# TensorE's instructions in phase 1 of a gated-DeltaNet layer: the scheduler's order against the order of emission

## The chip, the cores and the metric

One core of one Trainium2 chip runs the whole layer as one program. The metric is the device time of one execution in microseconds; for a profiled execution the profile also gives a span, from the first instruction of the core to the last.

## The reference, cut to what matters

One decoder layer, batch 1, 256 tokens, width 2048, everything in float32. The first half is the gated DeltaNet:

```python
mod = cond @ mod_w + mod_b                      # six vectors of 2048: sh1, sc1, ga1, sh2, sc2, ga2
h = x * (1 + sc1) + sh1
proj = h @ w_in                                 # 256 x 2048 by 2048 x 12352: q, k, v, z, beta, a
qkv = silu(causal_depthwise_conv(qkv, conv_w))  # 4 taps
q, k = l2norm(q) * 128 ** -0.5, l2norm(k)       # 16 heads of 128; v, z have 32 heads
# per value head, chunks of 64 in the reference (the kernel takes 128):
L = strict_lower((k * beta) @ k.T * decay)
u, w = solve(L + I, [v * beta, k * beta * exp(gc)])
# state recurrence over the chunks gives o
o = o * rsqrt(mean(o * o)) * norm_w * silu(z)
y = o @ w_out                                   # 4096 -> 2048
x = layer_norm(alpha * x + (1 + ga1) * y)
y = (silu(h2 @ w_gate) * (h2 @ w_up)) @ w_down  # SwiGLU, 5632 wide
out = layer_norm(alpha * x + (1 + ga2) * y)
```

## The kernel before, in words

**Products.** Every big matrix product is done in "groups" of 512 output columns (class `Group`, L194). A group walks over the 16 k-tiles of 128 in chunks of four. Each f32 weight tile is split into a rounded high part and a rest: ScalarE writes `wh` (L190), VectorE writes `wl` (L191), each 128 x 1024, for two k-tiles at once. One k-tile for one half `t` of the tokens is three matmuls of 512 columns (L223 to L225), here called three products. So a group is 96 products and one pair `wh`, `wl` serves 12 of them. There are four buffers each of `raw`, `wh` and `wl`, which is 48 products of lead. The variable `pos` counts chunks: one unit of it is 24 products. All times given to tasks are in this unit.

**Phases.** First come the modulation vectors and six groups that are interleaved with them (`first`), whose accumulators have the name `gd`. Phase 1 is the rest of the projection `w_in`: the loop over q = 1 to 3 (q, k and two v groups each) and the z groups, accumulators `pj`. Then the output projection (`oTa` and so on), the SwiGLU and the second norm follow. The change is in phase 1.

**Tasks.** Beside the products of phase 1 the kernel does the convolution and the DeltaNet for four batches q = 0 to 3 of eight value heads each. These are Python generators that `spawn` puts in a heap with a time in `pos`. `advance(t)`, called ahead of every three products, emits those steps that are due; `yield d` puts the rest of a task off by d. A task's step emits instructions on TensorE, VectorE, ScalarE and others at once. The steps that the prediction speaks of:

- `conv_silu`: four transposes into `tp` (L462), on VectorE six shifted multiply-adds `cy` (L470), Silu; later `qk_pair` transposes back (L494), `v_pair` (L529).
- `gates`: emitted once, ahead of phase 1. Transposes (L415), some twenty small VectorE and ScalarE operations ending in `q` (L443), then two matmuls (L445, L446).
- `la_task`: four per batch. ScalarE writes `dg` (L543), TensorE transposes it (L547), ScalarE takes the exponent `dm` (L551), TensorE multiplies k by k and q (L556), VectorE scales into `LA` (L561).
- `solve_task`: one per batch. ScalarE copies the diagonal blocks (L570), VectorE transposes them to `LD` (L573), then inverts 32 x 32 triangles in 31 dependent pairs of small operations (`tmp` L584, `X` L586) and transposes back to `XD` (L588). After a `yield` of SOLVE = 5.4 the small matmuls L600, L601 on `XD` follow, then further products (L608 to L627) with `yield HOP` between them.
- `state_task`: two per batch, matmuls L640 to L685, a `yield HOP` between most steps.
- `mods_late`: streams 96 tiles `mraw` of 128 x 1024 and adds each to `macc` on VectorE (L272, the first of 32 by L271), one per 0.95 `pos`; its sums go through L351 and L280.

**What sets the order.** Each engine runs its instructions in the order of its program, and waits at an instruction until what it needs is there. That order is made when the kernel is built. `at(p)` gives what is emitted inside it the priority p: lower first. A list scheduler goes through modelled time and gives each engine, whenever it is free, the ready instruction of lowest priority number. So an instruction of a task whose operand is late in the model lets products pass, and it comes on the engine when its operand is there in the model. The weight splits have a priority ten `pos` ahead (`SPLIT`) and so go before everything else as soon as a buffer is free.

Of the kernel before, what the change touches and what calls it, by code (L numbers as in the profile page):

```python
# [18 lines left out]
KT = D // 128  # L19
FF = 5632  # L20
FT = FF // 128
NQ = 4
# [7 lines left out]
def gdn_layer_kernel(ctx: ExitStack, tc: tile.TileContext, x, c, mod_w, mod_b, ln_g, ln_b,  # L30
# [3 lines left out]

    SPLIT, MOD0, MODEVERY = 10, 30.0, 0.95
    MGAP, CGAP0, CGAP, CSTEP = 1.5, 1.0, 2.0, 2.3
    CONV, PAIR, SILU = 0.2, 0.4, 2.4
    GDN, LAGAP, LA1, LA2, LA3, SOLVE, HOP = 3.0, 0.5, 0.3, 0.6, 1.5, 5.4, 0.6
    ALONE, MACW, ZW, OW = 1.5, 1.0, 0.1, 0.3


# [26 lines left out]
    def spawn(t, gen):  # L68
        heappush(tasks, (t, len(seq), gen))
        seq.append(gen)  # L70
# [3 lines left out]
    def drain(but=None):  # L74
        while any(x_[2] is not but for x_ in tasks):
            advance(now[0] + 0.1)

    def advance(t):
        now[0] = t
        while tasks and tasks[0][0] <= t:  # L80
            t0, i, gen = heappop(tasks)
            with at(t0):
                d = next(gen, None)
            if d is not None:
                heappush(tasks, (t0 + d, i, gen))
# [16 lines left out]
    w_in2 = w_in.rearrange("l k n -> (l k) n")  # L102
# [74 lines left out]
    pos = [0]  # L177
# [299 lines left out]
    def evac(t, ps):  # L477
        n = gp.tile([128, 512], F32, name="nat", tag="nat", bufs=4)
        act(n, ps, AF.Copy)
        return n  # L480

    def qk_pair(q, which, nat, h, ss, both):
        ct0 = (16 if which == 0 else 0) + q * 4
        while q > 1 and q - 2 not in state_ends:
            yield 0.2
        if q not in kq:
            kq[q] = gp.tile([128, 4, 2, 256], F32, name="kq", tag="kq", bufs=2)
        if which == 0 and q not in knat:
            knat[q] = gp.tile([128, 4, 128], F32, name="knat", tag="knat", bufs=2)
        yield from conv_silu(nat, h, ct0 + h, kq[q][:, h:h + 2, which, :])  # L490
        p = tp()
        for c in range(2):
            for i in range(2):
                tr(p[:, c * 256 + i * 128:c * 256 + (i + 1) * 128],  # L494
                   kq[q][:, h + i, which, c * 128:(c + 1) * 128], ident)
        if which == 0:
            act(knat[q][:, h:h + 2, :], p[:, 0:256].rearrange("p (a b) -> p a b", a=2), AF.Copy)
        for c in range(2):
            for i in range(2):
                src = p[:, c * 256 + i * 128:c * 256 + (i + 1) * 128]  # L500
                act(src, src, AF.Square, accum_out=ss[:, c, h + i:h + i + 1])
        both.append(h)

    def qk_norm(q, which, ss, both):
        while len(both) < 2:
            yield 0.2
        ts(ss, ss, NORM_EPS, None, op0=OP.add)
        r = work.tile([128, 2, 4], F32, name="rn", tag=f"rn{which}", bufs=2)
        nc.gpsimd.tensor_tensor(r.rearrange("p a b -> p (a b)"), ss.rearrange("p a b -> p (a b)"),
                                mhalf[:, 0:8], op=OP.pow)  # L510
        r2 = work.tile([128, 2, 4, 2], F32, name="rr", tag=f"rr{which}", bufs=2)
        ts(r2, r[:, :, :, None].to_broadcast([128, 2, 4, 2]), 1.0 if which == 0 else QSCALE, None, op0=OP.mult)
        (rk2 if which == 0 else rq2)[q] = r2.rearrange("p a b c -> p a (b c)")
        if which == 0:
            i2 = work.tile([128, 2, 4, 2], F32, name="ik", tag="ik", bufs=2)
            tt(i2, r2, ss[:, :, :, None].to_broadcast([128, 2, 4, 2]), op=OP.mult)
            ik2[q] = i2.rearrange("p a b c -> p a (b c)")
        return
        yield

    def v_pair(q, half, nat, h):
        ct0 = 32 + q * 8 + half * 4
        vT = yield from conv_silu(nat, h, ct0 + h, None)
        while q not in ik2:
            yield 0.2
        p = tp()
        for c in range(2):
            for i in range(2):
                tr(p[:, c * 256 + i * 128:c * 256 + (i + 1) * 128], vT[:, i, c * 128:(c + 1) * 128], ident)  # L529
        hq = half * 4 + h  # L530
        for c in range(2):
            for i in range(2):
                act(oq[q][:, c, hq + i, :], p[:, c * 256 + i * 128:c * 256 + (i + 1) * 128], AF.Copy,
                    scale=ik2[q][:, c, hq + i:hq + i + 1])
# [156 lines left out]
    def gdn(q):  # L691


        while q not in rq2 or q and q - 1 not in state_ends:
            yield 0.2
        hv, rk, rq = q * 8, rk2[q], rq2[q]
        LA[q] = gp.tile([128, 16, 2, 128], F32, name="LA", tag="LA", bufs=1)
        sc = work.tile([128, 2, 2, 8], F32, name="gsc", tag="gsc", bufs=2)
        tt(sc[:, 0], rk, rk, op=OP.mult)
        tt(sc[:, 0], sc[:, 0], beta[:, :, hv:hv + 8], op=OP.mult)  # L700
        tt(sc[:, 1, 0], sc[:, 0, 0], kse[:, hv:hv + 8], op=OP.mult)
        for c in range(2):
            for g in range(2):
                spawn(now[0] + LAGAP * (2 * c + g), la_task(q, c, g, sc))
        yield 3 * LAGAP + LA3
        yield from solve_task(q)
        omq[q] = work.tile([128, 2, 8], F32, name="om", tag="om", bufs=2)
        spawn(now[0] + 0.3, state_task(q, 1, sc))
        yield from state_task(q, 0, sc)
        while state_done.get(q) != 2:  # L710
            yield 0.1
        state_ends.add(q)
        f = work.tile([128, 2, 8], F32, name=f"fo{q}", tag=f"fo{q}", bufs=1)
        t = work.tile([128, 2, 8], F32, name="ft", tag="ft", bufs=1)
        tt(t, rq, rq, op=OP.mult)
        tt(t, t, omq[q], op=OP.mult)
        ts(t, t, 1.0 / 128.0, NORM_EPS, op0=OP.mult, op1=OP.add)
        nc.gpsimd.tensor_tensor(f.rearrange("p a b -> p (a b)"), t.rearrange("p a b -> p (a b)"), mhalf, op=OP.pow)
        tt(f, f, rq, op=OP.mult)
        fo[q] = f  # L720
# [3 lines left out]
    def conv_start():  # L724
        t = max(now[0] + CONV, conv_free[0])
        conv_free[0] = t + CSTEP
        return t

    def qk_done(q, which):
        nat = []  # L730

        def done(t, ps, n=None):
            nat.append(evac(t, ps) if n is None else n)
            if t == 0:
                return
            both = []
            ss = work.tile([128, 2, 4], F32, name="ss", tag="ss", bufs=2)
            t1 = conv_start()
            for h in (0, 2):
                spawn(t1 + PAIR / 2 * h, qk_pair(q, which, nat, h, ss, both))  # L740
            spawn(t1 + PAIR + SILU + 0.6, qk_norm(q, which, ss, both))
        return done

    def v_done(q, half):
        nat = []

        def done(t, ps, n=None):
            nat.append(evac(t, ps) if n is None else n)
            if t == 0:
                return  # L750
            if q not in oq:
                oq[q] = held.tile([128, 2, 8, 128], F32, name=f"oq{q}", tag=f"o{q}")
            t1 = conv_start()
            for h in (0, 2):
                spawn(t1 + PAIR / 2 * h, v_pair(q, half, nat, h))
            if half == 1:
                spawn(t1 - CONV + GDN, gdn(q))
        return done
# [149 lines left out]
    def late_mods():  # L908
        yield from mods_late(ga1, 32, 1.0, MODEVERY)
        yield from mods_late(sc2, 64, 1.0, MODEVERY)  # L910
        yield from mods_late(sh2, 48, 0.0, MODEVERY)
        tt(A2, lng[:, 0:KT], sc2, op=OP.mult)
        tt(B2, lnb[:, 0:KT], sc2, op=OP.mult)
        tt(B2, B2, sh2, op=OP.add)
# [3 lines left out]
    mods_gen = late_mods()  # L918
    spawn(MOD0, mods_gen)

    def z_group(q, half):
        Group(w_in2, 8192 + q * 1024 + half * 512, h_hi, h_lo, KT, z_done(q, half)).run()

    for q in range(1, NQ):
        if q > 1:
            Group(w_in2, 2048 + q * 512, h_hi, h_lo, KT, qk_done(q, 0)).run()
            Group(w_in2, q * 512, h_hi, h_lo, KT, qk_done(q, 1)).run()
        for half in range(2):
            Group(w_in2, 4096 + q * 1024 + half * 512, h_hi, h_lo, KT, v_done(q, half)).run()
        if q == 1:  # L930
            z_group(0, 0)
    for z in range(1, 2 * NQ):
        z_group(z // 2, z % 2)
    z1 = pos[0]
    drain(mods_gen)

    with at(z1 - 2):
        r = [held.tile([128, D], F32, name=f"r{t}", tag=f"h{t}") for t in range(2)]
# [194 lines left out]
```

## Time and profile before

| | us |
|---|---|
| median of 3 runs | 1722.5 (1720.7 to 1725.71) |
| the profiled execution | 1725.16 |
| its span | 1723.4 |
| TensorE busy | 1668.0 (97% of the span) |
| VectorE busy | 1139.7 (66%) |
| ScalarE busy | 882.0 (51%) |
| DMA, mean | 227 GB/s |

Matmuls overlap in the pipeline (a product is listed with some 390 to 400 ns and the next starts after 228 ns), so TensorE's busy share says that it seldom waits, not that it is at its peak. Phase 1 lies between about 218 and 780 us.

### The profile page before, as it was taken

Reading aid. Unit: us, or ns where it says so; the run is one execution under the profiler, and the core shown is the slowest. Engines: PE = TensorE matmul, PEld = TensorE weight load, DVE = VectorE, ACT = ScalarE, POOL = GpSimd, SP = SyncE. Lnnn points to the kernel's source line nnn. Section 1 sums busy time; section 2 is a strip of 40 time slices with the busy share of each in tenths; the row PEclk is TensorE's granted clock in tenths of the full one; section 3 lists DMA queues with packets and bytes.
Section 4 is the critical chain, followed back from the end, with each engine's and each line's share of the span. In section 5 each row is a group of like instructions: output and inputs, shape, how many; then the busy total and the mean of one; then the engine's idle time right before and its main releaser. Section 6 shows DMA issues by size and latency. Waiting matters only on the chain.

```text
span 1723.4 us, 23269 instructions
## 1 busy us (share of the span) xinstructions
PE 1668.0 (97%) x8685; PEld 1325.3 (77%) x8685; DVE 1139.7 (66%) x1635; ACT 882.0 (51%) x1430; POOL 61.2 (4%) x66
## 2 busy tenths in 40 slices
PE   5999999999999999999999999999999999999996
PEld 2666778787887878788787788888878887888885
DVE  2466988958966988847776865865467544455455
ACT  2433669769568667564333744444444443433332
POOL 0000000001001000000000000000000000000003
PEclk8999999999999999999999999999999999999998
DMA  9998786535864777747888586886678666756662
GB/s 347 364 338 286 223 283 191 170 112 159 255 204 117 241 251 241 245 147 238 302 278 282 158 270 185 304 268 189 189 246 284 191 185 207 249 192 192 196 193 101
DMA packets 184082, 390.82 MB, mean 227 GB/s; under 512 B 12112, under 2 KB 14592, under 8 KB 182944
## 3 DMA queue, kind: packets, MB, share of 16 engines
q1 hardware_dynamic: 181952, 378.64, 67.7%
q0 software_dynamic: 2016, 10.68, 1.8%
q8 instruction: 68, 1.11, 0.3%
q14 instruction: 46, 0.38, 0.1%
HBM read 385.08 MB, written 4.19 MB: 226 GB/s over the span
## 4 chain that ended last, share of the span: by engine, by line
PE 70%; DVE 12%; DMA 7%; ACT 5%; issue 4%; POOL 1%; SPq 1%; POOLq 0%; DVEq 0%; ACTq 0%
PE pj L223 19%; PE pj L225 19%; PE pj L224 19%; DMA mraw<-in_mod_w_dram 6%; DVE wl L191 5%; ACT wh L190 2%; PE gd L225 1%; PE gd L224 1%; DVE macc L272 1%; DVE cy L470 1%; PE gd L223 1%; DVE X L586 1%; DVE tmp L584 1%; PE tp L311 1%; PE tp L1039 1%
## 5 line engine op out<-in xcount | busy, mean ns | idle before, releaser
L191 DVE TENSOR_TENSOR wl<-raw,wh 128x1024 fp32r<-128x1024 f32 x522 | 635.1, 1222 | 376.7 <-ACT wh L190 374.1
L190 ACT ACTIVATE wh<-raw 128x1024 fp32r<-128x1024 f32 x522 | 552.3, 1061 | 602.4 <-PE pj L225 481.1
L223 PE MATMUL pj<-wh,h2T 128*128 128x512 f32 x704 | 278.2, 395 | 0.0
L225 PE MATMUL pj<-wh,h2T 128*128 128x512 f32 x704 | 276.7, 393 | 0.0
L224 PE MATMUL pj<-wl,h2T 128*128 128x512 f32 x704 | 276.5, 393 | 0.0
L223 PE MATMUL pj<-wh,hT 128*128 128x512 f32 x640 | 256.8, 403 | 0.0
L224 PE MATMUL pj<-wl,hT 128*128 128x512 f32 x640 | 256.5, 401 | 0.1
L225 PE MATMUL pj<-wh,hT 128*128 128x512 f32 x640 | 256.2, 401 | 0.0
L272 DVE SCALAR_TENSOR_TENSOR macc<-mraw,cond,macc 128x1024 f32<-128x1024 f32 x120 | 153.6, 1280 | 54.6 <-DMA mraw<-in_mod_w_dram 53.9
L223 PEld LDWEIGHTS pj<-wh,h2T 128*128 128x128 f32 x704 | 132.8, 189 | 30.5 <-issue 1.6
L225 PEld LDWEIGHTS pj<-wh,h2T 128*128 128x128 f32 x704 | 132.7, 189 | 28.7 <-issue 0.8
L224 PEld LDWEIGHTS pj<-wl,h2T 128*128 128x128 f32 x704 | 132.7, 188 | 27.8 <-issue 0.8
L223 PEld LDWEIGHTS pj<-wh,hT 128*128 128x128 f32 x640 | 120.8, 189 | 26.7 <-issue 3.3
L224 PEld LDWEIGHTS pj<-wl,hT 128*128 128x128 f32 x640 | 120.8, 189 | 24.5 <-DVE wl L191 0.9
L225 PEld LDWEIGHTS pj<-wh,hT 128*128 128x128 f32 x640 | 120.9, 189 | 24.4 <-issue 1.2
L470 DVE SCALAR_TENSOR_TENSOR cy<-tp,cw,cy 128x255 f32<-128x255 f32 (+2 forms) x192 | 86.2, 476 | 1.3 <-ACT cy L466 1.2
L224 PE MATMUL gd<-wl,hT 128*128 128x512 f32 x128 | 51.5, 404 | 1.4 <-DVE wl L191 1.4
L223 PE MATMUL gd<-wh,hT 128*128 128x512 f32 x128 | 49.9, 398 | 2.0 <-DVE part L256 1.1
L225 PE MATMUL gd<-wh,hT 128*128 128x512 f32 x128 | 51.8, 408 | 0.0
L311 PE MATMUL tp<-mraw,cond 128*32 128x256 f32 x368 | 34.9, 464 | 11.4 <-DMA mraw<-in_mod_w_dram 11.4
L223 PE MATMUL pj<-wh,oTc 128*128 128x512 f32 x112 | 43.9, 392 | 0.0
L225 PE MATMUL pj<-wh,oTc 128*128 128x512 f32 x112 | 43.8, 391 | 0.0
(388 smaller groups left out, 2266.3 us busy)
## 6 DMA issues: line engine op xcount, KB each, us to landing
raw<-in_gdn_w_in_dram SPq DMA_DIRECT2D x194, 512.0 KB, 4.6
mraw<-in_mod_w_dram SPq DMA_DIRECT2D x192, 512.0 KB, 5.4
raw<-in_ffn_w_gu_dram SPq DMA_DIRECT2D x176, 512.0 KB, 4.3
raw<-in_ffn_w_down_dram SPq DMA_DIRECT2D x88, 512.0 KB, 4.6
raw<-in_gdn_w_out_dram SPq DMA_DIRECT2D x64, 512.0 KB, 5.1
x<-in_x_dram SPq DMA_DIRECT2D x8, 256.0 KB, 5.9
r<-in_x_dram POOLq DMA_DIRECT2D x2, 1024.0 KB, 5.0
x1s<-r POOLq DMA_DIRECT2D x2, 1024.0 KB, 6.8
```

The costliest lines, as they stand in the source:

```text
L190: act(hi, raw, AF.Copy)
L191: tt(lo, raw, f32(hi), op=OP.subtract)
L223: mm(ps, sh, wh, start=start, stop=False)
L224: mm(ps, sh, wl, start=False, stop=False)
L225: mm(ps, sl, wh, start=False, stop=stop)
L272: return stt(acc, w, cond[:, k:k + 1], acc, op0=OP.mult, op1=OP.add)
L311: mm(p[32 * j:32 * j + 32, 0:hw], cond[:, k:k + 1].to_broadcast([128, 32]), raw[:, kl, j * hw:(j + 1) * hw], start=(k == 0), stop=(k == KT ...
L470: stt(y[:, o + s:o + 256], p[:, o:o + 256 - s], tap(3 - s, ct + i), y[:, o + s:o + 256], op0=OP.mult, op1=OP.add)
L584: tt(tv, LD[:, j + 1:32, j:j + 1].to_broadcast([128, n, m]), X[:, j, None, 0:m].to_broadcast([128, n, m]), op=OP.mult)
L586: tt(X[:, j + 1:32, 0:m], X[:, j + 1:32, 0:m], tv, op=OP.subtract)
L1039: tr(p[:, i * 256 + t * 128:i * 256 + (t + 1) * 128], nats[j, t][:, (2 * i2 + i) * 128:(2 * i2 + i + 1) * 128], ident)
```

## The change

The region `manual_schedule` for TensorE is put around the loops of phase 1. Inside it TensorE's instructions keep the order in which they are emitted: all of a step's TensorE instructions stand in one place, at the `pos` at which the task was due, and the products behind them stay behind them. The other engines are ordered by the scheduler as before. Four constants of the task times are changed too: the convolution starts 0.45 instead of 0.2 `pos` after its group, LA1 goes from 0.3 to 0.5, HOP from 0.6 to 0.7. SOLVE stays at 5.4.

```diff
-    CONV, PAIR, SILU = 0.2, 0.4, 2.4
-    GDN, LAGAP, LA1, LA2, LA3, SOLVE, HOP = 3.0, 0.5, 0.3, 0.6, 1.5, 5.4, 0.6
+    CONV, PAIR, SILU = 0.45, 0.4, 2.4
+    GDN, LAGAP, LA1, LA2, LA3, SOLVE, HOP = 3.0, 0.5, 0.5, 0.6, 1.5, 5.4, 0.7
...
-    for q in range(1, NQ):
...
-    z1 = pos[0]
-    drain(mods_gen)
+
+    with tc.manual_schedule(engines={mybir.EngineType.PE}):
+        for q in range(1, NQ):
+            if q > 1:
+                Group(w_in2, 2048 + q * 512, h_hi, h_lo, KT, qk_done(q, 0)).run()
+                Group(w_in2, q * 512, h_hi, h_lo, KT, qk_done(q, 1)).run()
+            for half in range(2):
+                Group(w_in2, 4096 + q * 1024 + half * 512, h_hi, h_lo, KT, v_done(q, half)).run()
+            if q == 1:
+                z_group(0, 0)
+        for z in range(1, 2 * NQ):
+            z_group(z // 2, z % 2)
+        z1 = pos[0]
+        drain(mods_gen)
```

What this moves is seen in the order of the built programs. The first place is TensorE at the start of phase 1, where the gates are computed; L415 writes the transposes that the chain of small operations starts from, L445 takes that chain's result `q`. Before, around L415 and then around L445, with 83 products between the two:

```order
L223 MATMUL pj<-wh,hT_116 128x512
L415 MATMUL tp<-ident,bT 128x64 x2
L224 MATMUL pj<-wl,hT_116 128x512
L225 MATMUL pj<-wh,hT_118 128x512
```

```order
L224 MATMUL pj<-wl,hT_117 128x512
L225 MATMUL pj<-wh,hT_119 128x512
L445 MATMUL tp<-q,upper 128x64
L446 MATMUL tp<-q,upper 128x32
L462 MATMUL tp<-ident,part 128x128 x4
L223 MATMUL pj<-wh,hT_117 128x512
```

The same place in the change, where the last row ahead of L415 is the last product of the six first groups:

```order
L223 MATMUL gd<-wh,hT_117 128x512
L224 MATMUL gd<-wl,hT_117 128x512
L225 MATMUL gd<-wh,hT_119 128x512
L415 MATMUL tp<-ident,bT 128x64 x2
L445 MATMUL tp<-q,upper 128x64
L446 MATMUL tp<-q,upper 128x32
L462 MATMUL tp<-ident,part 128x128 x4
L223 MATMUL pj<-wh,hT_116 128x512
L224 MATMUL pj<-wl,hT_116 128x512
```

No product stands between L415 and L445 any more: the first convolution of the region (L462) comes behind L446 as it did before, and the products of the region come behind that convolution.

The second place is VectorE ahead of the second `XD` (batch q = 1). Before, the end of that inversion with the weight splits and convolutions between its pairs:

```order
L272 SCALAR_TENSOR_TENSOR macc<-mraw,cond,macc 128x1024
L586 TENSOR_TENSOR X<-X,tmp 128x6x13
L470 SCALAR_TENSOR_TENSOR cy<-tp,cw_102,cy 128x255
L584 TENSOR_TENSOR tmp<-LD,X 128x70
L470 SCALAR_TENSOR_TENSOR cy<-tp,cw_102,cy 128x255
L586 TENSOR_TENSOR X<-X,tmp 128x5x14
L191 TENSOR_TENSOR wl<-raw,wh 128x1024
L584 TENSOR_TENSOR tmp<-LD,X 128x56
L191 TENSOR_TENSOR wl<-raw,wh 128x1024
L586 TENSOR_TENSOR X<-X,tmp 128x4x14
```

And in the change, the end of the same inversion:

```order
L584 TENSOR_TENSOR tmp<-LD,X 128x56
L272 SCALAR_TENSOR_TENSOR macc<-mraw,cond,macc 128x1024
L586 TENSOR_TENSOR X<-X,tmp 128x4x14
L584 TENSOR_TENSOR tmp<-LD,X 128x45
L272 SCALAR_TENSOR_TENSOR macc<-mraw,cond,macc 128x1024
L586 TENSOR_TENSOR X<-X,tmp 128x3x15
L584 TENSOR_TENSOR tmp<-LD,X 128x30
L586 TENSOR_TENSOR X<-X,tmp 128x2x15
L584 TENSOR_TENSOR tmp<-LD,X 128x16
L586 TENSOR_TENSOR X<-X,tmp 128x16
L588 STREAM_TRANSPOSE XD<-X 128x32x16
```

The last weight split of this stretch now stands some 36 rows ahead of `XD`, and `macc` stands where splits and convolutions stood.

The third place is TensorE at the same solve, between the last L556 of the batch's four la tasks and the first L600. Before, 283 products stand between the two, and the L600s may cut a group of three:

```order
L224 MATMUL pj<-wl,hT_116 128x512
L225 MATMUL pj<-wh,hT_118 128x512
L223 MATMUL pj<-wh,hT_116 128x512
L224 MATMUL pj<-wl,hT_116 128x512
L225 MATMUL pj<-wh,hT_118 128x512
L223 MATMUL pj<-wh,hT_116 128x512
L600 MATMUL gd<-XD,LA 32x32
L601 MATMUL gd<-XD,LA 32x32
```

In the change 141 products stand between the two, in whole threes, with six steps of four transposes (the last an L529) and one pair of L351 and L280:

```order
L529 MATMUL tp<-ident,cy 128x128 x4
L223 MATMUL pj<-wh,hT_117 128x512
L224 MATMUL pj<-wl,hT_117 128x512
L225 MATMUL pj<-wh,hT_119 128x512
L223 MATMUL pj<-wh,hT_117 128x512
L224 MATMUL pj<-wl,hT_117 128x512
L225 MATMUL pj<-wh,hT_119 128x512
L223 MATMUL pj<-wh,hT_117 128x512
L224 MATMUL pj<-wl,hT_117 128x512
L225 MATMUL pj<-wh,hT_119 128x512
L600 MATMUL gd<-XD,LA 32x32
L601 MATMUL gd<-XD,LA 32x32
```

The solve moved ahead by 142 products relative to its la tasks. For the four batches the number of products between the last L556 and the first L600 goes from 228, 283, 255 and 230 to 138, 141, 138 and 174. Between the same marks VectorE's program (from the first of the last four L561 to L588) holds, before: 18, 23, 21, 19 splits `wl`; 42, 36, 36, 0 multiply-adds `cy`; 0, 11, 7, 8 `macc` of L272. In the change: 11, 12, 13, 15 splits; 24, 12, 24, 0 `cy`; 0, 13, 11, 5 `macc`. Over the whole program the places at which TensorE goes from a product to something else go from 308 to 286.

## Rows read from the trace of the kernel before

**Rows 1.** The page's part 1, TensorE: busy us (share of the span), instructions.

```profile
PE 1668.0 (97%) x8685; PEld 1325.3 (77%) x8685; DVE 1139.7 (66%) x1635; ACT 882.0 (51%) x1430; POOL 61.2 (4%) x66
```

**Rows 2.** TensorE's waits at 212 to 790 us: total us, times, longest us.

```profile
PE tp L445 <- DVE q L443: 2.5, 1, 2.5
...
PE gd L600 <- DVE XD L588: 2.1, 3, 1.7
```

**Rows 3.** TensorE's timeline in phase 1: start us, us, what, count.

```profile
422.20 0.40 PE L223 MATMUL pj<-wh,hT 128*128 128x512 f32 x1
...
422.58 0.66 PE L462 MATMUL tp<-ident,nat 128*128 128x128 f32 x4
...
422.99 0.48 PE L224 MATMUL pj<-wl,hT 128*128 128x512 f32 x1
...
424.61 0.39 PE L225 MATMUL pj<-wh,hT 128*128 128x512 f32 x1
...
431.89 0.39 PE L224 MATMUL pj<-wl,hT 128*128 128x512 f32 x1
```

**Rows 4.** Stretches from last L556 step to first L600, one per batch.

```profile
core 0: us, PE busy (x) PEld busy (x) DVE busy (x) ACT busy (x) POOL busy (x), PEclk, DMA share, GB/s
290.67:351.93 61.26, 60.34 (x287) 48.06 (x286) 54.99 (x137) 46.51 (x105) 3.27 (x2) 1.00 0.54 156
411.20:485.30 74.10, 73.24 (x349) 58.50 (x348) 71.13 (x151) 47.97 (x92) 4.24 (x2) 1.00 0.77 243
541.18:609.59 68.41, 66.77 (x321) 53.16 (x319) 65.03 (x143) 46.43 (x97) 3.27 (x2) 1.00 0.71 221
668.20:725.03 56.83, 55.11 (x251) 45.31 (x249) 55.38 (x118) 29.42 (x33) 0.00 (x0) 1.00 0.80 255
```

**Rows 5.** VectorE's groups, first of these stretches: busy us, mean ns | idle.

```profile
L191 DVE TENSOR_TENSOR wl<-raw,wh 128x1024 fp32r<-128x1024 f32 x19 | 23.2, 1224 | 4.5 <-ACT wh L190 4.4
...
L470 DVE SCALAR_TENSOR_TENSOR cy<-tp,cw,cy 128x255 f32<-128x255 f32 (+2 forms) x42 | 19.8, 481 | 0.0
```

**Rows 6.** The same in the second stretch.

```profile
L191 DVE TENSOR_TENSOR wl<-raw,wh 128x1024 fp32r<-128x1024 f32 x23 | 27.9, 1218 | 0.4 <-ACT wh L190 0.3
...
L470 DVE SCALAR_TENSOR_TENSOR cy<-tp,cw,cy 128x255 f32<-128x255 f32 (+2 forms) x36 | 17.1, 475 | 0.0
...
L272 DVE SCALAR_TENSOR_TENSOR macc<-mraw,cond,macc 128x1024 f32<-128x1024 f32 x12 | 15.3, 1274 | 0.4 <-DMA mraw<-in_mod_w_dram 0.4
```

**Rows 7.** TensorE's timeline around the gates.

```profile
219.49 0.33 PE L415 MATMUL tp<-ident,bT 64*128 64x64 f32 x2
...
241.31 0.41 PE L445 MATMUL tp<-q,upper 128*128 128x64 f32 x2 [2.45 <-DVE q L443]
```

**Rows 8.** VectorE's timeline of the gates: first and last of 29 rows.

```profile
220.58 0.28 DVE L417 COPY ba<-tp 128x128 f32<-128x128 f32 x1
...
240.95 0.22 DVE L443 SCALAR_TENSOR_TENSOR q<-q,nA 128x64 f32<-128x64 f32 x1
```

**Rows 9.** A stretch with la tasks; columns as in rows 4.

```profile
245.00:300.00 55.00, 54.95 (x274) 44.28 (x273) 47.31 (x81) 54.62 (x115) 3.57 (x4) 1.00 0.67 211
```

**Rows 10.** ScalarE's groups at 245 to 780 us: busy us, mean ns | idle.

```profile
L190 ACT ACTIVATE wh<-raw 128x1024 fp32r<-128x1024 f32 x140 | 148.3, 1061 | 69.0 <-PE pj L225 53.1 <-issue 10.6 <-DMA raw<-in_gdn_w_in_dram 2.3
...
L543 ACT ACTIVATE dg<-below,gc 128x128 f32<-128x128 f32 x63 | 20.9, 407 | 0.0
...
L551 ACT ACTIVATE dm<-gd,ngc 128x128 f32<-128x128 f32 x64 | 19.0, 372 | 1.2 <-PE gd L547 1.1
```

**Rows 11.** TensorE's wait at 958 to 962 us.

```profile
PE tp L967 <- DVE hf L975: 2.9, 1, 2.9
```

**Rows 12.** Stretches of that wait and behind it; columns as in rows 4.

```profile
958.20:961.50 3.30, 0.44 (x2) 0.01 (x1) 3.27 (x10) 3.30 (x9) 0.84 (x2) 0.88 0.70 240
961.50:967.50 6.00, 5.96 (x16) 4.59 (x17) 6.00 (x14) 4.87 (x9) 0.31 (x1) 0.50 0.56 203
```

More of the change, by code (lines that the diff above doesn't have):

```diff
@@ L922, in z_group @@
         Group(w_in2, 8192 + q * 1024 + half * 512, h_hi, h_lo, KT, z_done(q, half)).run()
-    for q in range(1, NQ):
[L925 to L933, printed above, removed]
-    z1 = pos[0]
-    drain(mods_gen)
+    with tc.manual_schedule(engines={mybir.EngineType.PE}):
[11 more added lines that the diff above has]
+        drain(mods_gen)
     with at(z1 - 2):
```

## The prediction

> **What bounds the kernel now.** I read the page's busy shares first. TensorE is busy 97% of the span [rows 1], so what it does not wait for cannot be won, and what it is made to wait for is lost. Next I asked how much there is to win where the change acts: in the list of TensorE's waits in phase 1 the two largest are 2.5 us for the gates' `q` at L445 and 2.1 us, over three solves, for `XD` at L600 [rows 2]. The other entries are of 1.4 us and less. So before, TensorE hardly waits at all. Then the pace: in the timeline 32 products take from 424.61 to 431.89 us, 0.2275 us each, and a step of four transposes between two products takes 422.99 - 422.20 - 0.2275 = 0.56 us [rows 3].
>
> The reason that it hardly waits is read from the stretches between the last L556 of a batch and its first L600. They last 61.3, 74.1, 68.4 and 56.8 us, and in them not only TensorE but VectorE too is nearly full: 54.99, 71.13, 65.03 and 55.38 us [rows 4]. VectorE has the splits (1.22 us each), the convolution (0.48 us each) and the inversion's 31 pairs to do [rows 5, 6]. It is the inversion on VectorE that lasts so long, and TensorE fills the time with 228 to 283 products. That is the cover which the order gave.
>
> **What the change adds, leg by leg.** In the change TensorE comes to L600 after 138, 141, 138 and 174 products. Its way there, products at 0.2275, steps at 0.56 (8, 6, 6 and 0 of four transposes, and in the last three an L351 and an L280 counted as two more) and 0.6 for the last L556 step itself: 31.4 + 4.5 + 0.6 = 36.5; 32.1 + 3.4 + 1.1 + 0.6 = 37.2; 31.4 + 3.4 + 1.1 + 0.6 = 36.5; 39.6 + 1.1 + 0.6 = 41.3 us. The same sum for the first stretch before (228 products, 13 steps) gives 59.8 against the measured 61.26 [rows 4], so the way is priced right within 1.5 us.
>
> VectorE's way to `XD` I get from the measured stretch by taking off what no longer stands ahead of `XD` in its program and adding what now does. It keeps the four L561, the transposes and the 31 pairs. At 1.22 us for a split, 0.48 for a `cy`, 1.27 for a `macc` [rows 5, 6]:
>
> - batch 0: 7 splits and 18 `cy` fewer: 61.3 - 8.5 - 8.6 = 44.2, TensorE waits 7.7 us;
> - batch 1: 11 splits and 24 `cy` fewer, 2 `macc` more: 74.1 - 13.4 - 11.4 + 2.5 = 51.8, wait 14.6;
> - batch 2: 8 splits and 12 `cy` fewer, 4 `macc` more: 68.4 - 9.8 - 5.7 + 5.1 = 58.0, wait 21.5;
> - batch 3: 4 splits and 3 `macc` fewer: 56.8 - 4.9 - 3.8 = 48.1, wait 6.8.
>
> Together 50.6 us, of which 2.1 were there before: **+48.5**. Behind L600 stand the products and every later step of TensorE, so each of these microseconds moves the end. The splits do not help: with four buffers they can be 48 products ahead and then stop until TensorE goes on. If the pairs wait for each other longer than the difference shows, or the `macc` for their loads, it is more; if the stretch before held idle time of VectorE that goes away (6.3 us in batch 0, 3.0, 3.4 and 1.5 in the others, span minus busy in [rows 4]), it is up to 14 less. Bounds +34 and +60.
>
> **The gates.** From L415 to L445 it is 241.31 - 219.49 = 21.8 us now, covered by 83 products [rows 7]. VectorE's part of it is the 29 rows from L417 to L443 [rows 8]; by the order, six splits and five `macc` are among them, in the change no split and three `macc`. 21.8 - 6 x 1.22 - 2 x 1.27 = 11.9 us with no product left to cover them. TensorE waits some 11.5 us instead of 2.5, and the seven products that stood ahead of L415 at the start of phase 1 are gone from there too (1.6 us more until its operand comes): **+10.5**. Bounds: +7 if half of the remaining `macc` wait goes, +13 if the ScalarE links of the chain, hidden under splits now, come to the surface.
>
> **The la tasks.** ScalarE has 16 `dg` and 16 `dm` per batch, 16 x (0.407 + 0.372) = 12.5 us, and a `wh` of 1.06 us for each 12 products [rows 10]; where a batch's la tasks run it is full, 54.62 of 55 us in the stretch that holds the first [rows 9]. In the change the four tasks stand 12 products apart, 51 products and eight steps from first L547 to last L556, some 16 us, in which ScalarE's 12.5 + 5 x 1.06 = 17.8 and what else stands among them (convolution copies, squares, table loads) do not quite fit. I estimate 3 us a batch, **+12**, between 0 (if `dg` is written well ahead) and 22.
>
> **The state steps.** Two state tasks with the two `gd` buffers stand six products (1.4 us) apart; before, products slipped in while a buffer was read out. I take 2 us a batch, **+8**, between 0 and 12: no row shows a wait there now, the nearest being the readers' own sub-microsecond operations.
>
> **The clock.** At 958.2 us TensorE waits 2.9 us at L967 [rows 11]; the granted clock falls within that stretch of 3.3 us to a mean of 0.88, and the next 6.0 us run at 0.50, the 1.2 GHz level, with 16 matmuls where full speed has some 26 products' time [rows 12]. The longest wait in phase 1 now, 2.5 us, left no such mark. Five new waits (gates and four solves) are longer than that one. Half of 6.0 us would be 3.0 each; as small matmuls and short steps stand first behind L600, I take 2.5: **+12.5**, between 0 and 18 (if some la waits count too).
>
> The Trainium skill, in "TensorE: Matmul & The Clock Gate", section "HAM oscillation — how this bites in real kernels", says that idle gaps between bursts of matmuls put the clock back to half rate and that the loss is half of the time spent there, paid again at each burst. It speaks against this change; rows 12 agree (0.50 for 6.0 us behind one wait). By its half, the term would be 15 instead of 12.5.
>
> **What the change saves.** 22 fewer entries into a step. Four transposes have as many columns as one product, so of the 0.56 us some 0.33 is the entering: at most 22 x 0.33 = 7; as many of the removed entries split off single transposes, I take **-3**. The moved constants cost nothing themselves: HOP and CONV add 0.1 and 0.25 `pos`, 0.5 and 1.4 us, to chains that products cover.
>
> Sum: 48.5 + 10.5 + 12 + 8 + 12.5 - 3 = +88.5 us. The profiled execution of 1725.16 us becomes 1813.7; against the median of 1722.5, **1811 us**. The part after phase 1 keeps its order of phases and its bound and should keep its time.
>
> **Rivals.**
>
> 1. *Faster.* The fixed order goes through without stopping and only the entries (7 us) and the two large waits (4.6 us) go: 1711 us. It decides at one point, VectorE's way to `XD`: it must be no longer than TensorE's 36.5 us. The four L561, the transposes and the 31 pairs alone are some 21 us, so 15 us are left for the rest, a dozen splits. The program holds 11 to 15 splits and 24, 25, 35 and 21 other large or middling operations there. Chance 3%.
> 2. *Only VectorE's legs and the gates.* ScalarE keeps up, `gd` frees in time, the clock does not fall: 48.5 + 10.5 - 3 = 56, 1778 us; with the legs at their lower bound 1764. For it: where TensorE has waited, ScalarE has caught up. Against it: rows 9 and rows 12. Chance 20%.
> 3. *The waits add up further.* The la and state terms at their upper bounds, the clock falling more often, and the `macc` that now stand ahead of `XD` one after another (13 and 11 in batches 1 and 2) waiting for their loads, since `mraw` has only two buffers: VectorE's legs at +60: 60 + 13 + 22 + 12 + 18 = 125, 1847 us. Chance 15%.
> 4. *No difference,* because what VectorE does early while TensorE waits is saved later: it would need a later stretch in which VectorE is the bound. Behind L600 VectorE has the splits and short reads alone, so TensorE sets the pace there. Chance 2%.
>
> **How the numbers follow.** The forecast case has 60%, with its own range 1785 to 1835; rivals 2 and 3 have 35% between them and set the ends: 1768, a little over rival 2's lower end, and 1857, a little over rival 3. 0.3% (5 us) is about what a measurement of this kernel tells from no change. Slower 0.95 (forecast, 2 and 3), same 0.02, faster 0.03.
>
> **What would show it.** In the profile of the changed kernel: L600 waiting for `XD` (L588) at the head of TensorE's waits, four times, some 50 us together, the third the longest; one wait of about 11 us at L445 for L443; 0.50 in the granted clock behind them; VectorE's stretch from the last L556 to `XD` at 44 to 58 us instead of 57 to 74. Phase 1 would end some 85 to 90 us later and all after it be shifted alone. The forecast is wrong if VectorE has `XD` ready ahead of TensorE, or if L600's waits are there and phase 1 ends on time all the same, for then something other than TensorE's order was its bound.

## The result, and the profile after

The change takes 1874.3 us (1871.4 to 1875.2) against 1723.4 us of the kernel before in the same rounds (1720.7 to 1725.7), a ratio of 1.087 [1.085, 1.089]. I had forecast 1811 us with a range up to 1857. The sign and the main wait were right, the size was not: +151 us in place of +88.5.

The page of the kernel after, part 1, answers to [rows 1]:

```profile
PE 1698.5 (91%) x8685; PEld 1350.4 (72%) x8685; DVE 1151.1 (61%) x1635; ACT 890.1 (48%) x1432; POOL 59.5 (3%) x66
```

The span is 1873.4 us. TensorE stands idle for 1873.4 - 1698.5 = 174.9 us, 119.5 more than before (1723.4 - 1668.0 = 55.4), and is busy 30.5 us longer with the same 8685 instructions. VectorE and ScalarE do the work they did, in a longer time.

TensorE's waits in phase 1 (236 to 925 us), in which [rows 2] had 2.5 and 2.1 us at the head:

```profile
PE gd L600 <- DVE XD L588: 58.2, 4, 23.7
PE tp L445 <- DVE q L443: 10.7, 1, 10.7
PE gd L670 <- DVE oq L666: 7.5, 4, 2.4
PE gd L547 <- ACT dg L543: 7.3, 6, 1.9
PE tp L494 <- DVE X L586: 4.7, 1, 4.7
PE gd L547 <- DVE LA L561: 4.3, 2, 2.2
PE gd L556 <- ACT dm L551: 3.7, 3, 1.7
PE tp L529 <- DVE cy L470: 3.4, 2, 2.1
```

Then the stretches from the last L556 of a batch to its first L600 (answering to [rows 4]), each followed by the one up to the next batch's last L556:

```profile
core 0: us, PE busy (x) PEld busy (x) DVE busy (x) ACT busy (x) POOL busy (x), PEclk, DMA share, GB/s
304.74:355.90 51.16, 38.48 (x175) 30.68 (x173) 44.54 (x119) 29.49 (x68) 3.27 (x2) 0.95 0.43 124
355.90:446.47 90.57, 79.83 (x573) 64.75 (x574) 41.55 (x77) 64.15 (x142) 4.09 (x4) 0.95 0.32 94
446.47:508.80 62.33, 40.38 (x183) 31.98 (x181) 53.75 (x116) 27.38 (x69) 3.70 (x2) 0.83 0.68 214
508.80:594.20 85.40, 77.89 (x571) 63.52 (x571) 42.03 (x71) 60.49 (x142) 3.77 (x4) 0.96 0.40 116
594.20:659.98 65.78, 39.80 (x180) 31.70 (x178) 56.84 (x127) 29.63 (x66) 3.27 (x2) 0.81 0.64 197
659.98:747.14 87.16, 79.80 (x569) 65.06 (x570) 41.58 (x69) 59.39 (x140) 3.84 (x4) 0.93 0.39 117
747.14:799.49 52.35, 41.82 (x191) 33.79 (x190) 46.61 (x108) 22.30 (x26) 0.00 (x0) 0.96 0.69 213
```

Two things are to be seen. In the solves' stretches VectorE is busy for 44.5, 53.8, 56.8 and 46.6 us, which are nearly the 44.2, 51.8, 58.0 and 48.1 us of my sum; but the stretches last 51.2, 62.3, 65.8 and 52.4. I had priced VectorE's work and taken it for its way. And in the stretches between, no engine is full: TensorE is busy for 88 to 92% of them, and the smaller rows of its waits above name ScalarE and VectorE by turns.

What VectorE waits for in the third of the solves' stretches (594.2 to 660 us):

```profile
DVE rr L512 <- POOL rn L509: 2.9, 2, 1.6
DVE LA L561 <- PE gd L556: 2.9, 1, 2.9
DVE macc L272 <- DMA mraw<-in_mod_w_dram: 1.8, 3, 0.8
DVE wl L191 <- ACT wh L190: 1.7, 1, 1.7
```

And in the third stretch before (541.2 to 609.6 us):

```profile
DVE rr L512 <- POOL rn L509: 1.4, 1, 1.4
DVE wl L191 <- ACT wh L190: 0.9, 2, 0.5
DVE macc L272 <- DMA mraw<-in_mod_w_dram: 0.8, 2, 0.6
```

These are small links to GpSimd, TensorE, ScalarE and the DMA queues, and in the change each is longer. Over the four stretches VectorE's idle time is 6.6 + 8.6 + 8.9 + 5.7 = 29.8 us (stretch less busy), twice the 6.3 + 3.0 + 3.4 + 1.5 = 14.2 us before.

Phase 1 carries nearly all of the loss: the first product of the output projection starts at 910.2 us (before 765.8, +144.4), and from there to the end it is 963 us against 958. Of the 144.4 us, 19.8 are there at the 577th product of the groups, the first of phase 1: it starts at 237.5 us in place of 217.7. In the change it stands behind the gates' L415 and L445, which wait 1.6 and 10.7 us.

### The profile page after: what moved, and what is told of

Its sections match the earlier page's. It is cut to its first block, busy times and chain, and to the rows that moved or that the text cites. A ratio compares the mean times of both kernels' runs of the same rounds, so it can differ in the third digit from the quotient of the medians.

```text
span 1873.4 us, 23251 instructions
## 1 busy us (share of the span) xinstructions
PE 1698.5 (91%) x8685; PEld 1350.4 (72%) x8685; DVE 1151.1 (61%) x1635; ACT 890.1 (48%) x1432; POOL 59.5 (3%) x66
## 4 chain that ended last, share of the span: by engine, by line
PE 65%; DVE 13%; DMA 8%; ACT 6%; issue 6%; POOL 1%; SPq 1%; POOLq 0%; DVEq 0%; ACTq 0%
PE pj L223 17%; PE pj L224 17%; PE pj L225 17%; DMA mraw<-in_mod_w_dram 7%; DVE wl L191 5%; ACT wh L190 2%; DVE macc L272 2%; DVE cy L470 1%; PE gd L225 1%; PE gd L224 1%; PE gd L223 1%; DVE X L586 1%; PE tp L311 1%; DVE tmp L584 1%; ACT tp L501 1%
## 5 line engine op out<-in xcount | busy, mean ns | idle before, releaser
L223 PE MATMUL pj<-wh,hT 128*128 128x512 f32 x640 | 275.1, 432 | 0.0
L225 PE MATMUL pj<-wh,hT 128*128 128x512 f32 x640 | 256.9, 402 | 0.0
L272 DVE SCALAR_TENSOR_TENSOR macc<-mraw,cond,macc 128x1024 f32<-128x1024 f32 x120 | 153.6, 1280 | 62.9 <-DMA mraw<-in_mod_w_dram 62.2
L225 PEld LDWEIGHTS pj<-wh,hT 128*128 128x128 f32 x640 | 124.6, 195 | 29.0 <-issue 0.8
L223 PEld LDWEIGHTS pj<-wh,hT 128*128 128x128 f32 x640 | 125.9, 197 | 25.3 <-issue 2.5
L224 PEld LDWEIGHTS pj<-wl,hT 128*128 128x128 f32 x640 | 125.8, 197 | 23.2 <-DVE wl L191 0.9
L470 DVE SCALAR_TENSOR_TENSOR cy<-tp,cw,cy 128x255 f32<-128x255 f32 (+2 forms) x192 | 82.0, 473 | 6.1 <-ACT cy L466 6.0
L600 PE MATMUL gd<-XD,LA 32*32 32x32 f32 x128 | 7.6, 236 | 58.2 <-DVE XD L588 58.2
L225 PE MATMUL gd<-wh,hT 128*128 128x512 f32 x128 | 52.4, 412 | 0.0
L600 PEld LDWEIGHTS gd<-XD,LA 32*32 32x32 f32 x128 | 7.1, 151 | 59.9 <-DVE XD L588 49.4
L311 PE MATMUL tp<-mraw,cond 128*32 128x256 f32 x368 | 35.4, 470 | 10.9 <-DMA mraw<-in_mod_w_dram 10.9
```

The costliest lines, as they stand in the source:

```text
L223: mm(ps, sh, wh, start=start, stop=False)
L224: mm(ps, sh, wl, start=False, stop=False)
L225: mm(ps, sl, wh, start=False, stop=stop)
L272: return stt(acc, w, cond[:, k:k + 1], acc, op0=OP.mult, op1=OP.add)
L311: mm(p[32 * j:32 * j + 32, 0:hw], cond[:, k:k + 1].to_broadcast([128, 32]), raw[:, kl, j * hw:(j + 1) * hw], start=(k == 0), stop=(k == KT ...
L470: stt(y[:, o + s:o + 256], p[:, o:o + 256 - s], tap(3 - s, ct + i), y[:, o + s:o + 256], op0=OP.mult, op1=OP.add)
```

## Experiments

Every run has the kernel before beside it; it took 1725.0 us in the first set (constants, region, SOLVE 7.6, late region), 1723.0 in the second (dummies, fewer `macc`, pinned solves) and 1728.8 in the third (the rest). Runs with an interval have four and more executions, the others one; where a kernel ran four times or more, its times lie within 4 to 10 us of each other, so a difference of a few us between two single runs is not told from none.

**Which edit costs it: the constants or the order?** `e1_consts` has the changed constants without the fixed order (CONV, LA1 and HOP; they are three, not four as I wrote of the change), `e2_region_oldconsts` the fixed order with the constants of before.

```diff
-    CONV, PAIR, SILU = 0.2, 0.4, 2.4
-    GDN, LAGAP, LA1, LA2, LA3, SOLVE, HOP = 3.0, 0.5, 0.3, 0.6, 1.5, 5.4, 0.6
+    CONV, PAIR, SILU = 0.45, 0.4, 2.4
+    GDN, LAGAP, LA1, LA2, LA3, SOLVE, HOP = 3.0, 0.5, 0.5, 0.6, 1.5, 5.4, 0.7
```

> The kernel before with the changed constants (CONV 0.45, LA1 0.5, HOP 0.7) alone; the scheduler still orders TensorE. Theory (the fixed order costs the time): 1723 us, within 0.5% of before, no wait of TensorE over 3 us in phase 1. Rival (the later task times cost a good part, since each batch's chain gets longer): 1740 to 1780 us.

> The region for TensorE alone, with the constants of before. Theory: as slow as the change, 1860 to 1895 us; the first solves' waits like those of the change (some 55 us at L600 together), and somewhat more waits behind the hops and the convolutions, whose places come 0.1 and 0.25 pos earlier. Rival (constants): clearly nearer to before, 1760 to 1820 us.

Measured: the constants alone 1747.0 us, 1.013 [1.011, 1.016], 22 us slower, as the rival had it; the order alone 1852.5, 127.5 slower, a little under the 1860 to 1895 expected. 22 + 127.5 = 149.5, the whole of the change: the two add up. The order alone has the main waits of the change (150 to 960 us):

```profile
PE gd L600 <- DVE XD L588: 46.4, 4, 20.3
PE gd L547 <- ACT dg L543: 15.0, 9, 5.0
PE tp L445 <- DVE q L443: 11.2, 1, 11.2
```

So my sentence that the moved constants cost nothing was wrong by 22 us, and the order costs 39 us more than the 88.5 I gave it. With the constants of before the fixed order reaches the first batch's last L556 at 289.3 us in place of 304.7, behind nearly as many products (753 and 756), and at the fourth solve's L600 it is 20.9 us ahead of the change: most of the constants' cost lies ahead of the first solve.

**Which constant?** `e13_conv` has CONV 0.45 alone, `e14_la1_hop` LA1 0.5 and HOP 0.7 alone, in the free order.

> The kernel before, with one constant of the change alone: CONV 0.45 in place of 0.2 (a later place for the first groups' convolution steps); no fixed order. All three constants without the order cost 22 us. Theory A: the cost sits here, because the first solves' inputs come later; 1735 to 1745 us, with L600's waits for XD still under 6 us. Theory B: it sits in LA1 and HOP; within 5 us of the kernel before (1718 to 1729).

> The other half: LA1 0.5 and HOP 0.7 in place of 0.3 and 0.6, CONV as before, no fixed order. Theory A (CONV carries the 22 us): within 6 us of the kernel before. Theory B (each la task and each state hop stands later, so every pass takes longer): 1740 to 1750 us. The two halves should add up to 22 us, give or take 4.

Measured: CONV 1742.8 us, 1.0084 [1.0062, 1.0106], +14.0; LA1 and HOP 1735.5, 1.0040 [1.0025, 1.0056], +6.8. Together 20.8, as expected of the halves. Both cost, CONV two thirds. TensorE's waits with CONV alone (150 to 960 us) have a new head:

```profile
PE tp L462 <- DVE cy L470: 5.1, 1, 5.1
...
PE gd L600 <- DVE XD L588: 2.4, 3, 1.5
```

It lies at some 190 us, ahead of phase 1, and the 577th product of the groups, where phase 1 begins, starts at 225.2 us in place of 217.7. That is half of CONV's cost; the solves are unharmed.

**Do the constants pay the other way round?** `e15_early`: CONV 0.0, LA1 0.1, HOP 0.5, free order.

> A candidate against both kernels: no fixed order, CONV 0.0, LA1 0.1, HOP 0.5, the three constants moved the other way. If the scheduler puts a step that comes too early behind products that can run, as the runs so far suggest, earlier places cost nothing and win part of what later ones lost: 1705 to 1718 us. Rival: the constants before are at a flat bottom or early places begin to wait: 1722 to 1740 us.

Measured 1735.1 us, 1.0044 [1.0027, 1.0060]: slower too. The rival holds: moved together, the three constants win in neither direction. Each of them moved early by itself was not tried.

**Are the solves alone enough?** `e11_pin_solve` is the kernel before, whose scheduler stays free, with one thing fixed: each batch's first L600 stays behind the products emitted ahead of it, and the next 48 calls of three products stay behind that L600. `e12_pin_solve9` is the same with SOLVE 9.0 in place of 5.4, which puts L600 later.

```diff
-                    self.product(self.ps[t], k, t, kl, w, k == 0, k == self.nk - 1)
+                    with ExitStack() as behind:
+                        if first600:
+                            ins = first600[0]
+                            behind.enter_context(tc.issue_after(ins.ins))
...
+                        self.product(self.ps[t], k, t, kl, w, k == 0, k == self.nk - 1)
...
+            if s == 0:
+                first600.append(tc.keep_in_program_order(ins))
```

> The kernel before, with its constants and the scheduler's order, but each batch's first L600 is kept behind the products emitted ahead of it and the next 144 products behind it: only the solves stand at a fixed place, 62, 115, 99 and 164 products behind the last L556. Theory (the wait is VectorE's way less TensorE's way, and it is lost): ways of VectorE of 45, 56, 56 and 53 us less ways of TensorE of 19, 31, 27 and 39 give waits of some 94 us, and with 10 us of clock 1815 to 1835. Rival (half of such a wait comes back, because the scheduler moves other work of TensorE ahead of it): 1765 to 1785.

> The same with SOLVE 9.0, 133, 175, 165 and 259 products. Theory: ways of VectorE of 51, 67, 53 and 44 us less 35, 44, 41 and 61 give waits of 16, 23, 12 and 0, 50 us, and some 1775 to 1790 us; the later solves of batch 3 end some 100 products later, which costs up to 15 us at the end of phase 1. Rival (the place of the solve matters little): as e11, within 15 us.

Measured: 1828.6 and 1803.0 us, 105.6 and 80.0 over the kernel before beside them. The first time is inside its expectation, but not for its reason: that had some 94 us of waits at L600, and there are 53.7. The second is above its expectation and outside the rival's 15 us. TensorE's waits of the first (its L609 is L600, its L538 is L529, its L794 is L783):

```profile
PE gd L609 <- DVE XD L597: 53.7, 4, 24.8
PE tp L538 <- ACT cy L482: 16.9, 4, 7.1
PE tp L794 <- DVE oTa L829: 5.5, 1, 5.5
```

and of the second (its L360 is L351):

```profile
PE gd L609 <- DVE XD L597: 27.9, 3, 11.3
PE tp L360 <- DVE macc L281: 14.7, 1, 14.7
```

Between the two, L600's waits fall by 25.8 us and the time by 25.6. That the two agree is luck in part: L529's wait for `cy` goes as well (16.9 to 2.0 us), a new one of 14.7 us comes at L351 just ahead of the second L600, and with the later solves work moves behind the start of the output projection: its first product comes 62 us earlier (807.9 in place of 870.3), the rest takes 37 us longer (993.3 in place of 956.5). And the wait shown at L600 is only half of what a pinned solve costs: 105.6 us for 51.6 us more of waiting there. The first has 62, 115, 99 and 164 products between a last L556 and its L600, the second 133, 175, 165 and 259. The order alone has 141, 141, 141 and 180 (the change 138, 141, 138 and 174), between the two but for the first batch, and its 46.4 us at L600 lie between theirs. So I estimate that of the 127.5 us of the order the four solves' places alone make some 80 to 105, and that the la tasks, the state steps, the gates and all other places are left with 22 to 47. That the parts add up in this way is not shown, since the scheduler orders everything else anew around a pinned solve.

**Later solves within the fixed order.** `e3_solve76` is the change with SOLVE 7.6.

> The change with SOLVE 7.6 instead of 5.4, so that 189, 192, 192 and 225 products stand between the last L556 and the first L600 instead of 138, 141, 138 and 174. Theory (L600 stands too early for VectorE): each solve gets some 11.5 us of cover, less what VectorE does more in that time; L600's waits fall from 58 to about 35 us, and with fewer half-clock stretches the time falls by 25 to 35 us, to 1840 to 1850. Rival (VectorE bounds phase 1 and the place does not matter): L600's waits fall but others rise, 1865 to 1880 us.

Measured 1891.3 us, 17 slower than the change; neither expectation held. TensorE's waits (150 to 970 us):

```profile
PE gd L600 <- DVE XD L588: 28.9, 3, 11.2
PE tp L462 <- DVE cy L470: 17.9, 3, 8.6
PE tp L280 <- ACT sums L277: 15.1, 4, 5.9
PE tp L445 <- DVE q L443: 11.1, 1, 11.1
PE tp L462 <- ACT nat L479: 8.6, 1, 8.6
```

L600 waits 29.3 us less, as meant; in the other rows L462 and L280 wait 34 us more than in the change (4.8 us for `cy`, 3.0 for `sums`, none for `nat`). Its idle time is 1889.5 - 1711.9 = 177.6 us against the change's 174.9. A like move (SOLVE 9.0) went with 25.6 us won where only the solves were fixed; here it wins nothing: the next late operand takes over. Half of the loss lies behind the start of the output projection: its first product comes 7.3 us later (917.5), and from there to the end it takes 972.0 us in place of 963.2. Which move of tasks would avoid that was not found.

**The fallen clock behind the solves.** `e5_dummy` is the change with 16, 72, 94 and 34 products more, whose results are written over, ahead of the four L600 (L603 here), to fill the waits.

```diff
-        ppv = gd().rearrange("p (s c) -> p s c", s=16)
+        pp_ = gd()
+        for i in range((16, 72, 94, 34)[q]):
+            mm(pp_, hT[0, 0][:, i % 8, 0:128], hT[0, 1][:, 0:2, :].rearrange("p a b -> p (a b)"), start=True, stop=True)
+        ppv = pp_.rearrange("p (s c) -> p s c", s=16)
```

> The change with 16, 72, 94 and 34 products of 512 columns more, of no use, directly ahead of the four solves' first L600, written to the accumulator that L600 then overwrites: 3.6, 16.4, 21.4 and 7.7 us of work inside waits of 5.9, 18.5, 23.7 and 10.0 us. They take no time of their own and keep TensorE busy. Theory (the clock lost behind the solves is a small part, 2 to 3 us each): 6 to 12 us faster than the change, 1862 to 1868, with the half-clock stretches of 20.5 and 23.9 us gone. Rival (the fallen clock is what made the loss larger than forecast, 25 us and more): 1850 or less.

Measured 1872.5 us, 1.8 less than the change and inside the spread of its four executions; neither expectation held. The waits were filled:

```profile
PE gd L603 <- DVE XD L588: 8.8, 4, 2.7
```

The first 6.1 us behind the second solve and the next 15.1, in the change and then with the dummies:

```profile
508.80:514.90 6.10, 6.10 (x74) 5.17 (x75) 3.34 (x4) 5.60 (x9) 0.00 (x0) 0.50 0.57 173
514.90:530.00 15.10, 15.10 (x204) 12.41 (x204) 9.51 (x16) 10.79 (x17) 0.87 (x3) 1.00 0.48 137
```

```profile
509.40:515.50 6.10, 5.03 (x83) 3.92 (x83) 4.31 (x4) 5.97 (x9) 0.00 (x0) 1.00 0.56 186
515.50:530.60 15.10, 13.98 (x197) 11.78 (x197) 8.74 (x16) 10.45 (x17) 0.87 (x3) 1.00 0.45 133
```

The granted clock is 0.50, the 1.2 GHz level, in the one and 1.00 in the other, and after 21.2 us both have run nearly the same number of matmuls, 278 and 280 by these rows. At full clock TensorE merely stands idle in between, for ScalarE is full there (5.60 and 5.97 of 6.10 us), mostly with reading the solve's results out. Behind the four solves in turn, the 278th matmul from L600 on comes 0.8 and 0.2 us earlier, 0.4 later and 1.7 earlier than in the change. The clock falls behind the solves as I had forecast, and it costs nearly nothing there. The stretches up to the next last L556 do not become shorter (90.2, 87.1 and 89.4 us); but their mean granted clock does not rise either (0.96, 0.96 and 0.92), since it falls later in them, at 553 and 580 us for one. What a fallen clock costs between the solves is so left open.

**A shorter way on VectorE.** `e7_nomac` is the change without 15 of every 16 of the late modulation's tiles in phase 1, their loads and `macc`; it leaves out those parts of the sums for ga1, sc2 and sh2, so its time is one of less work.

> The change without 15 of every 16 of the late modulation tiles of phase 1 (their loads and their macc; it leaves out these parts of the sums for ga1, sc2 and sh2). Theory (the macc that stand ahead of XD lengthen VectorE's way): the ways to XD get shorter by 0, 15.6, 12.8 and 7.3 us, L600's waits fall from 58 to 25 to 30 us, mostly in batches 1 and 2, and the time by 30 to 40 us, to 1834 to 1844. Rival (the macc only fill gaps between dependent pairs of the inversion): L600's waits fall by less than 10 us, 1860 to 1874.

Measured 1822.7 us, 51.6 less than the change, more than the 30 to 40 expected. L600's waits fall from 58.2 us to (its L603 is L600):

```profile
PE gd L603 <- DVE XD L591: 21.8, 4, 10.7
```

The four stretches fall from 231.6 us to 51.2 + 46.4 + 51.2 + 44.0 = 192.8, and 10 us are won ahead of phase 1. VectorE is what the solves wait for. In the change its L272 are busy for 0, 16.6, 14.2 and 6.4 us in these stretches, 37.3 in all, and the stretches fall by 0, 15.9, 14.6 and 8.4, 38.8 in all: the work of the `macc` comes back whole, and their loads, which went too, leave little to be won. Over the whole kernel VectorE is busy 1151.1 - 1048.5 = 102.6 us less, of which half comes back as time.

**Where the fixed order begins.** `e4_late_region` is the change, `e9_late_oldconsts` the fixed order with the constants of before, begun one group later, so that 71 products stand between L415 and L445 in the first and 83 in the second.

```diff
+    Group(w_in2, 5120, h_hi, h_lo, KT, v_done(1, 0)).run()
     with tc.manual_schedule(engines={mybir.EngineType.PE}):
...
-            for half in range(2):
+            for half in range(1 if q == 1 else 0, 2):
```

> The change with the region begun one group (96 products) later, so that 71 products stand between L415 and L445 again; the rest of the order is that of the change. Theory: the wait of 10.7 us at L445 and the half-clock stretch of 13.7 us around it go, 12 to 16 us, 1858 to 1863. Rival (the wait moves to the next step that hangs on VectorE, since the batch's chain is what bounds): under 5 us gained, 1870 to 1875.

> The fixed order with the constants of before, begun one group later. Begun as in the change it took 1852.5 us; one group later won 8.4 us with the new constants. If the two are independent: 1844 us (1840 to 1848). Rival, the start of the order costs something only with the late CONV: 1850 to 1855 us.

Measured: 1865.9 us, 8.4 less than the change, between the two expectations; and 1856.2, where 1844 was expected and the rival had 1850 to 1855. The second is 127.5 us over its kernel before, as much as the fixed order begun early. Yet the gates' wait, 11.2 us there, is gone from its list of TensorE's waits (150 to 960 us):

```profile
PE gd L600 <- DVE XD L588: 47.1, 4, 20.1
PE gd L547 <- ACT dg L543: 18.1, 9, 5.0
PE gd L670 <- DVE oq L666: 5.2, 4, 1.3
```

The first batch's last L556 comes at 287.3 in place of 289.3 us, and L547 waits 18.1 us in place of 15.0. So with the constants of before, taking away a wait of 11 us at L445 won 2 us here and nothing at the end; 3 us of it are seen again as waits of the la tasks for ScalarE. With the constants of the change the wait at L445 falls from 10.7 to 0.4 us, and the first batch's last L556 comes at 298.7 in place of 304.7 us. These 6 us stay through phase 1: the next three last L556 come 5.4 to 6.7 us earlier, the output projection 4.9. So the same wait was worth 6 us of phase 1 with one set of constants and none at its end with the other; why is not shown.

## Why the prediction was wrong

- **Solves, +48.5.** Right in mechanism, place and shape: L600 waits for `XD` four times, 58.2 us in all, the third the longest. The failed step is "VectorE's way to `XD` I get from the measured stretch by taking off what no longer stands ahead". It took off splits and convolutions at their busy time, and so let the idle time of VectorE stay as short as before, or go; it doubled. VectorE's ways came out at 231.6 us against 202.1 forecast, and its idle time in them is 29.8. The idle time was small links to other engines, as the third stretch shows; what makes them longer was not tested by itself. Only 7.6 us of that difference show at L600, since TensorE's own way there grew as well (231.6 - 58.2 = 173.4 us in place of 151.5), by some 13 us of waits for other operands and by the fallen clock. Measured against the 151.5 us of products and steps, the term is 80, not 50.6, and my upper bound of +60 was too low.
- **la tasks, state steps.** The waits are there as named: L547 and L556 some 17 us, L670, L654 and L662 some 14, against 12 and 8. Between solves I estimate TensorE's work at full clock as its busy time less (1 - PEclk) of the stretch: 75.3, 74.5 and 73.7 us. The stretches last 15.3, 10.9 and 13.5 longer, 39.7 in all, where my 3 for la, 2 for state and 2.5 for the clock gave 22.5. Other steps too (L494, L529, L280, L462, L783) now have waits of 1 to 5 us, which I had given nothing.
- **Gates, +10.5.** The row was read rightly: L445 waits 10.7 us and L415 1.6, with 2.5 before. What it is worth is less sure than I wrote: 6 us of phase 1 (8.4 of the whole) by the late start with the change's constants, 2 and then nothing with those of before.
- **Clock, +12.5.** The granted clock fell behind the gates and each solve, with 5.1 to 6.1 us of busy TensorE at 0.50 each time, as forecast. It also fell in the la stretches, where waits are of 2 us. But behind the four solves full clock won 2.3 us by the 278th matmul, where my term had 10, and 1.8 us at the end, which is not told from nothing. As a price of the solves' places the term was wrong in kind: the slow matmuls stand there in time that others set. At the gates it was not tested. The Trainium skill says in "TensorE: Matmul & The Clock Gate", section "HAM oscillation — how this bites in real kernels", that half of the time at the lower clock is lost. By that an estimate for the 6.1 us at 0.50 behind the second solve is 3 us; the measurement decides, and by it they are not lost, since the same matmuls are done after 21.2 us either way.
- **Constants, 0.** Wrong: 14.0 for CONV, 6.8 for LA1 and HOP. I had said that products cover them. For CONV, whose first steps stand ahead of phase 1, TensorE waits 5.1 us at L462 in the free order too.
- **Entries, -3.** No run tells it apart.

By the spans the miss is 150.0 - 88.5 = 61.5 us. By place 29.5 of it lie in the solves' stretches and 17.2 between them; the other 15 are left for what lies ahead of the first and behind the last, with the 7.5 us that CONV costs ahead of phase 1 among them. Of rival 3 ("the waits add up further", 1847 us) the direction was right; it had the `macc` waiting for loads as one more cause, and all those of a stretch together waited for 1.4 to 2.0 us. Rival 2 fell with the solves: the solves fixed alone cost 80 and 105 us at two places, not its 56 with the gates.

What stays open: why a pinned solve costs twice its wait. The half beyond L600 in `e11_pin_solve` is seen as waits at L529 and L783 and as 19 us more of busy TensorE, but no run took these away one by one. Nor is it shown how much of TensorE's 30.5 us more of busy time, in the change, is lost.

## What to carry to other kernels

A free order hides an engine that is nearly full by giving TensorE something else; before it is fixed, the way of that other engine is to be priced with its idle time, since its own small links to a third engine may lengthen, as they did here from 14.2 to 29.8 us, once the order no longer bends around them. Waits in a chain do not add up as a list shows them: take one away (the gates, the solves in `e3_solve76`) and see whether the next operand is late too. A wait's price is tested by moving that one step alone, as with the pinned solves, and by then reading the whole list again: there the step cost twice its own wait.

## Not expected of the hardware

The granted clock of phase 1 as a whole, in the change and then before:

```profile
236.00:925.00 689.00, 577.46 (x3472) 466.08 (x3473) 448.97 (x873) 411.84 (x884) 30.49 (x25) 0.92 0.51 156
```

```profile
241.00:790.00 549.00, 540.98 (x3432) 435.98 (x3433) 433.88 (x865) 397.18 (x867) 32.23 (x25) 1.00 0.62 195
```

A mean of 0.92 over 689 us, with a lower level of 0.50, means some 0.08 x 689 / 0.5 = 110 us at the 1.2 GHz level, where before the kernel stood at 2.4 GHz throughout in spite of a wait of 2.5 us. That is more than the five long waits account for. One such stretch follows a wait of 1.8 us, and no longer one is listed in the 20 us ahead of it:

```profile
282.86:293.05 10.19, 8.53 (x22) 6.01 (x22) 2.88 (x5) 6.09 (x16) 0.00 (x0) 0.50 0.34 101
```

Much of the 110 us is waiting: the eleven stretches at 0.50 between 228 and 805 us last 111.5 us together, and TensorE is busy for 60.7 of them:

```profile
sum 111.54, PE 60.70 PEld 48.92 DVE 78.38 ACT 44.22 POOL 0.76; mean PE 5.52 PEld 4.45 DVE 7.13 ACT 4.02 POOL 0.07
```

So the lower clock can have cost some 30 us at most (an estimate, half of 60.7); behind the second solve, where both levels were tried, it cost no time.
